# A paired product schedule with 81 instead of 90 seven-product steps, eight raw and five split tiles, and activation forms made in place

## The chip, the cores and the metric

The kernel runs on one core of one Trainium2 chip. The metric is the time of one execution on the device, in microseconds (us); a run is one execution, and the time before is the median of three.

## The reference

One encoder block on 256 tokens of width 4096, all float32:

```python
h = rms_norm(x, pre_norm_gain)
proj = h @ w_in                      # q, k, v, gate_a, indexer, z, xs, b, c, dt, merge_logits
y_a = sparse_attention(...) * silu(gate_a)          # 256 x 2048
y_b = ssd_mixer(...)                                # 256 x 2048
gates = sigmoid(merge_logits)                       # two gates of 4096 columns
merged = gates[0] * (y_a @ w_branch_attn) + gates[1] * (y_b @ w_branch_ssd)
x = x + rms_norm(merged @ w_out, post_norm_gain)
```

Nearly all arithmetic is in the four kinds of matrix product: the input projection, the merge-gate columns of it, the two branch projections and the output projection.

## The kernel before

**Splits.** Each float32 product is made of three matmuls on a split pair: a high part (ScalarE copy into `wh`, rounded) and a low part (VectorE, value minus high part, `wl`); high x high, high x low and low x high are added up in PSUM. Weights come from HBM in raw tiles of 128 x 1024 (512 KB, `raw_tile`, RBUFS = 6 of them, line 26) on SP's DMA queue; their parts go to `wh` and `wl` tiles, SBUFS = 5 of each (line 25). A raw tile is free again when both parts are made.

**The first part** (`gemm`, lines 146 to 194, up to some 1609 us) does the indexer, the attention and the state-space projections and the first two gate blocks plainly, with attention and scan work fed in between.

**The paired part** (`pair_gemm`, lines 768 to 868) does the rest but for the last two blocks of the output projection. It works on two blocks of 512 output columns at once, on both halves of the tokens and on pairs `i` of 128-row blocks of the inner dimension: a 2 x 2 by 2 x 2 block product in each step. A step is of one of two kinds:

- S, seven products (a Winograd scheme, 21 matmuls of 128 x 128 by 128 x 512, all at L786). VectorE adds weight blocks for it (L830, L835, L836) ahead of the splits (L739 and L743, a last one of 512 columns).
- D, eight products, 24 matmuls, from differences of the activations; R is the same without differences. VectorE makes two low parts (L741 for the negated one, L743).

Which pairs are S is set by SX (gates: the odd pairs), SY (branches) and SM (output projection), lines 34 to 36, and by `plain` lists in which an S pair becomes R. The groups in order of time are called here G0 to G6 (seven gate groups, 16 steps each), B00, B01, B20 ... B61 (four column pairs n, two branches, 8 steps each) and O0, O2, O4 (output projection, 16 steps each). MIXED (line 881) is the order of the pairs in G0 to G5, O2 and O4: 0 to 7, then 9, 8, 11, 10, 13, 12, 15, 14. With odd pairs as S it reads D S D S D S D S S D S D S D S D. There are 90 S steps and 134 others.

**Banks.** Eight PSUM banks take the products; after each group `turn(mode)` maps the next group's products to the banks that are emptied first (LOG, line 749). `early`, `late` and `rest` (lines 788 to 814) empty them into four SBUF tiles with VectorE; L814 subtracts product 8.

**Activations.** For each pair, `make_base` splits the activation and `make_ext` (lines 700 to 719) forms its sums or differences into a tile `f` (name frm, one buffer) and splits them. The x inputs are formed before and in G0 (`ext_x`, L912), the branch inputs in G6 and B00 (read from HBM scratch, fr from yscr on POOL's queue, two fr tiles), those of the output projection from B61 on (fr from mscr).

**What sets the order.** Side work is written as generators on one list, `aux`; `step()` takes the next piece of the list's first generator, once or twice in each product step (`pace`), and that fixes the order of the program. The framework's planner then orders each engine's queue: by program order, but work that its own estimate of times holds ready may go ahead of earlier work that it holds not ready. At run time each queue is strictly in order. The loads of the gates (`load_sig`, L963) sit in SP's queue at step 5 of each branch group; `ev_branch` multiplies with them (L968), and its last use frees their tiles.

```python
            ra, rb = raw_tile(), raw_tile()
            load_half(ra, chunk(i), 0)
            load_half(rb, chunk(i), 1)
            if n in hooks:
                hooks[n]()
            if kind == "S":
                V.tensor_add(ra[:, 0, :], ra[:, 0, :], rb[:, 0, :])
                b11, b21 = split(rb, 2)
                t1, b22 = split(ra, 2)
                V.tensor_sub(ra[:, 1, :], ra[:, 0, :], ra[:, 1, :])
                V.tensor_sub(rb, rb, ra[:, 1:2, :].to_broadcast([P, 2, NW]))
                t2, = split(ra[:, 1:2, :], 1)
                t3, t4 = split(rb, 2)
```

Of the kernel before, what the change touches and what calls it, by code (L numbers as in the profile page):

```python
# [11 lines left out]
F32 = mybir.dt.float32  # L12
# [13 lines left out]
RBUFS = 6  # L26
# [7 lines left out]
SX = tuple(range(1, 16, 2))  # L34
# [10 lines left out]
def fused_block(tc, x, xT, w_qi, w_misc, w_attn, w_ssd, w_gate0, w_gate, w_br, w_out2, w_out,  # L45
# [304 lines left out]
    def transpose4(src, dst, eng):  # L350
# [4 lines left out]
        if eng is A:  # L355
            A.activation(dst, b3, AF.Copy)
        else:
            eng.tensor_copy(dst, b3)
# [13 lines left out]
    def qi_score(j):  # L372
        for t in range(2):
            nk = (t + 1) * P
            per = NW // nk
            for h0 in range(0, 8, 2 * per):
# [6 lines left out]
                for o in range(2):  # L383
                    rl = attp.tile([P, NW], F32, tag="rl", name="rl")
# [315 lines left out]
    def make_ext(i, a, seven, diff=True):  # L700

        n = 4 if i in seven else 2
        if n == 2 and not diff:
            return
        f = tp.tile([P, n, P], F32, tag="f", name="frm")
        if n == 4:
            a11, a21 = a[:, 0, 0:P], a[:, 0, P:S]
            a12, a22 = a[:, 1, 0:P], a[:, 1, P:S]
            V.scalar_tensor_tensor(f[:, 0, :], a22, -1.0, a21, ALU.mult, ALU.subtract)
            V.tensor_sub(f[:, 2, :], a21, a11)  # L710
            V.scalar_tensor_tensor(f[:, 1, :], f[:, 0, :], -1.0, a11, ALU.mult, ALU.subtract)
            V.tensor_sub(f[:, 3, :], f[:, 1, :], a12)
        else:
            V.tensor_sub(f, a[:, :, 0:P], a[:, :, P:S])
# [11 lines left out]
    def form(i, name):  # L726
        n = int(name[1])
        if name[0] == "S":
            return ext[i][:, 0, n - 1, :], ext[i][:, 1, n - 1, :]
# [38 lines left out]
    def pair_gemm(what, mode, chunk, plan, outs, evac, hooks={}, pace=1):  # L768
# [25 lines left out]
        def late():  # L794
# [4 lines left out]
            V.tensor_add(dest[1], ps[5], dest[1])  # L799
            V.scalar_tensor_tensor(dest[3], ps[5], -1.0, dest[2], ALU.mult, ALU.subtract)  # L800

        def rest():
# [7 lines left out]
            V.scalar_tensor_tensor(c12, ps[3], -1.0, c12, ALU.mult, ALU.subtract)  # L810
            V.tensor_add(c11, ps[2], c11)
            V.tensor_add(c21, ps[4], c21)
            if 8 in ps:
                V.tensor_sub(c22, c22, ps[8])  # L814
# [7 lines left out]
        for n, (i, kind) in enumerate(plan):  # L822
# [20 lines left out]
            else:  # L843
# [7 lines left out]
                if n == after:  # L851
                    early()
                    if not left.get(5):
                        late()
                        ended.append(0)
# [9 lines left out]
        if not ended:  # L865
            pending.append(late)
# [3 lines left out]
    def forms_from(what, load, seven, pairs, diff=True):  # L870
        a = load(pairs[0])
        for i in pairs:
            ahead = load(i + 1) if i + 1 in pairs else None
            make_base(i, a)
            make_ext(i, a, seven, diff)
# [3 lines left out]


    MIXED = (0, 1, 2, 3, 4, 5, 6, 7, 9, 8, 11, 10, 13, 12, 15, 14)
# [340 lines left out]
```

## Time and profile before

| what | value |
|---|---|
| median of three runs | 2918.04 us (2916.93 to 2919.03) |
| the profiled execution's own time | 2920.13 us |
| its span, first to last instruction | 2918.4 us |
| mean granted clock of TensorE | 0.995 of full speed |
| busy: TensorE, VectorE, ScalarE | 99%, 70%, 51% of the span |
| HBM traffic | 202 GB/s over the span |

Times in the profile are counted from the start of the span. A start is measured; the end of a matmul is modelled, and matmuls overlap, so a busy share of TensorE can hide short waits. PE is TensorE, PEld its weight loads, DVE VectorE, ACT ScalarE, SP and POOL the engines whose queues issue the DMAs. L786 is line 786 of the kernel. A row of the windows gives start and end, the length, the busy time of each engine with its number of instructions in brackets (PE, PEld, DVE, ACT, POOL as far as asked for), the granted clock of TensorE, the DMA engines' busy share and GB/s; a matmul of the group before that still runs at the start is in the number.

### The profile page before, as it was taken

To read this page: it belongs to the slowest core of one execution; us is meant where nothing else is said; L and a number is where in the kernel's file an instruction comes from. 1 tells how busy PE (TensorE), PEld (TensorE's weight loads), DVE (VectorE), ACT (ScalarE), POOL (GpSimd) and SP (SyncE) were. 2 spreads that over 40 slices of the span, in tenths; PEclk is the share of its full clock that TensorE was granted. 3 is DMA by queue.
4 is the path that set the end of the run, shared out by engine and by line. 5 is a ranking of instruction groups with operands and counts; after the bars stand their busy time and mean duration, and the time that the engine had idled before them with its cause. 6 is when DMAs were issued, how large, how long until landed. Compare 5 with 4: busy or idle time off the path is not lost.

```text
span 2918.4 us, 35378 instructions
## 1 busy us (share of the span) xinstructions
PE 2878.4 (99%) x12990; PEld 2364.6 (81%) x12990; DVE 2038.7 (70%) x2494; ACT 1490.1 (51%) x1805; POOL 197.9 (7%) x202
## 2 busy tenths in 40 slices
PE   9999999999999999999999999999999999999998
PEld 7878888888888888888888778787787888887876
DVE  6677455454554556565657888888897899988975
ACT  7444444444444445455545555555565555555553
POOL 0100001000010112121301000000000000000000
PEclk9999999999999999999999999999999999999999
DMA  9545555555555455545555566665676666865674
GB/s 358 186 161 179 188 179 191 192 179 189 180 189 193 176 185 177 186 175 186 177 185 193 182 222 215 210 215 198 206 240 233 230 237 228 277 219 184 225 244 151
DMA packets 170848, 592.40 MB, mean 203 GB/s; under 512 B 19632, under 2 KB 20400, under 8 KB 170672
## 3 DMA queue, kind: packets, MB, share of 16 engines
q1 hardware_dynamic: 163728, 567.05, 56.0%
q0 software_dynamic: 6944, 23.07, 2.2%
q8 instruction: 102, 1.67, 0.2%
q14 instruction: 74, 0.61, 0.1%
HBM read 570.12 MB, written 19.92 MB: 202 GB/s over the span
## 4 chain that ended last, share of the span: by engine, by line
PE 82%; DVE 8%; DMA 6%; issue 2%; ACT 1%; SPq 0%; DVEq 0%; ACTq 0%; POOLq 0%
PE p L786 25%; PE p L186 18%; PE p L188 18%; PE p L187 18%; DMA raw<-w_gate_d 3%; DVE wl L743 3%; DMA raw<-w_out_d 1%; ACT wh L739 1%; DVE raw L836 1%; DVE wl L741 1%; DMA fr<-yscr 1%; DVE raw L830 1%; PE p L353 1%; PE p L614 0%; PE p L381 0%
## 5 line engine op out<-in xcount | busy, mean ns | idle before, releaser
L178 DVE TENSOR_TENSOR wl<-raw,wh 128x1024 fp32r<-128x1024 f32 x560 | 696.6, 1245 | 593.7 <-ACT wh L177 591.8
L177 ACT ACTIVATE wh<-raw 128x1024 fp32r<-128x1024 f32 x560 | 593.7, 1061 | 791.3 <-PE p L188 696.2
L186 PE MATMUL p<-wh,b 128*128 128x512 f32 x2304 | 910.0, 395 | 1.4 <-ACT wh L174 1.1
L187 PE MATMUL p<-wl,b 128*128 128x512 f32 x2304 | 898.4, 390 | 0.2 <-DVE wl L175 0.2
L188 PE MATMUL p<-wh,b 128*128 128x512 f32 x2304 | 898.3, 390 | 0.0
L739 ACT ACTIVATE wh<-raw 128x1024 fp32r<-128x1024 f32 (+1 forms) x628 | 600.5, 994 | 454.6 <-DVE raw L835 202.8
L786 PE MATMUL p<-wh,b 128*128 128x512 f32 x2300 | 763.6, 393 | 2.4 <-ACT wh L739 1.5
L743 DVE TENSOR_TENSOR wl<-raw,wh 128x1024 fp32r<-128x1024 f32 (+1 forms) x494 | 544.0, 1123 | 59.1 <-ACT wh L739 57.4
L786 PEld LDWEIGHTS p<-wh,b 128*128 128x128 f32 x2300 | 434.9, 189 | 97.5 <-ACT wh L739 5.7
L186 PEld LDWEIGHTS p<-wh,b 128*128 128x128 f32 x2304 | 432.6, 188 | 93.4 <-ACT wh L174 3.3
L188 PEld LDWEIGHTS p<-wh,b 128*128 128x128 f32 x2304 | 432.4, 188 | 90.8
L187 PEld LDWEIGHTS p<-wl,b 128*128 128x128 f32 x2304 | 433.1, 188 | 88.7 <-DVE wl L175 1.4
L786 PE MATMUL p<-wl,b 128*128 128x512 f32 x1150 | 450.8, 392 | 2.2 <-DVE wl L741 2.1
L786 PE MATMUL p<-wh,ext 128*128 128x512 f32 x1104 | 388.0, 392 | 0.0
L786 PEld LDWEIGHTS p<-wl,b 128*128 128x128 f32 x1150 | 217.8, 189 | 49.2 <-DVE wl L741 2.8
L786 PEld LDWEIGHTS p<-wh,ext 128*128 128x128 f32 x1104 | 208.3, 189 | 44.4 <-ACT wh L739 2.5
L786 PE MATMUL p<-wl,ext 128*128 128x512 f32 x552 | 218.5, 396 | 17.3 <-DVE wl L743 17.0
L741 DVE SCALAR_TENSOR_TENSOR wl<-raw,wh 128x1024 fp32r<-128x1024 f32 x134 | 163.5, 1220 | 12.7 <-ACT wh L739 12.7
L786 PEld LDWEIGHTS p<-wl,ext 128*128 128x128 f32 x552 | 104.1, 189 | 47.2 <-DVE wl L743 26.2
L836 DVE TENSOR_TENSOR raw<-raw 128x1024 f32<-128x1024 f32 x90 | 110.1, 1223 | 2.0
L830 DVE TENSOR_TENSOR raw<-raw 128x512 f32<-128x512 f32 x90 | 62.1, 690 | 62.7 <-DMA raw<-w_gate_d 39.6
L290 POOL TENSOR_TENSOR ro<-m,m 128x512 f32<-128x512 f32 (+1 forms) x26 | 41.9, 1621 | 412.2 <-DVE m L288 404.1
(223 smaller groups left out, 1344.3 us busy)
## 6 DMA issues: line engine op xcount, KB each, us to landing
raw<-w_attn_d SPq DMA_DIRECT2D x256, 512.0 KB, 3.6
raw<-w_gate_d SPq DMA_DIRECT2D x256, 512.0 KB, 4.3
raw<-w_ssd_d SPq DMA_DIRECT2D x192, 512.0 KB, 3.6
raw<-w_br_d SPq DMA_DIRECT2D x128, 512.0 KB, 4.7
raw<-w_out_d SPq DMA_DIRECT2D x128, 512.0 KB, 4.7
raw<-w_qi_d SPq DMA_DIRECT2D x62, 512.0 KB, 5.3
sg<-sscr SPq DMA_DIRECT2D x32, 256.0 KB, 4.0
sscr<-pc POOLq DMA_DIRECT2D x28, 256.0 KB, 2.8
```

What stands on the lines that cost most here:

```text
L177: A.activation(wh, rs, AF.Copy)
L178: V.tensor_sub(wl, rs, wh.bitcast(F32))
L186: T.matmul(ps[t], al[:, tk], wh[:, i, :], start=first, stop=False)
L187: T.matmul(ps[t], ah[:, tk], wl[:, i, :], start=False, stop=False)
L188: T.matmul(ps[t], ah[:, tk], wh[:, i, :], start=False, stop=last)
L290: G.tensor_add(ro, m1, m2)
L739: A.activation(h, src, AF.Copy, scale=float(sign))
L741: V.scalar_tensor_tensor(l, src, -1.0, fbit(h), ALU.mult, ALU.subtract)
L743: V.tensor_sub(l, src, fbit(h))
L786: T.matmul(ps[j], l, r, start=first and n == 0, stop=left[j] == 0 and n == 2)
L830: V.tensor_add(ra[:, 0, :], ra[:, 0, :], rb[:, 0, :])
L836: V.tensor_sub(rb, rb, ra[:, 1:2, :].to_broadcast([P, 2, NW]))
```

## The change

- RBUFS goes from 6 to 8; SBUFS stays at 5. Room comes from smaller buffers elsewhere: `rl` (scores), `mT` (transposed merge results of the last block pair), `og` and the last residual tile use tiles that exist already.
- SX is 1, 3, 5, 8, 10, 12, 14, and MIXED is gone: the pairs come in plain order, D S D S D S D D S D S D S D S D. O0 has an order of its own. The S steps are 7 in each of six gate groups, 3 in G6, 18 in the branches, 4, 7 and 7 in O0, O2 and O4.
- `make_ext` forms the sums in the activation's own tile, without `f`; `forms_from` takes two list steps for each pair instead of one.
- The branch inputs are started at step 4 of G6, all 16 on one generator, instead of 8 at step 8 and 8 in B00. G6 hands its banks on in the mode "aux" instead of "D".
- `late`, `rest` and the end of a group take product 8 earlier in two cases.

```diff
-RBUFS = 6
+RBUFS = 8
...
-SX = tuple(range(1, 16, 2))
+SX = (1, 3, 5, 8, 10, 12, 14)
 SY = (1, 4, 6, 9, 12, 14)
 SM = SX
...
-                    rl = attp.tile([P, NW], F32, tag="rl", name="rl")
+                    rl = yr.tile([P, NW], F32, tag=f"yr{6 + o}", name="rl")
...
     def make_ext(i, a, seven, diff=True):
 
-        n = 4 if i in seven else 2
-        if n == 2 and not diff:
+        if i not in seven and not diff:
             return
-        f = tp.tile([P, n, P], F32, tag="f", name="frm")
-        if n == 4:
-            a11, a21 = a[:, 0, 0:P], a[:, 0, P:S]
-            a12, a22 = a[:, 1, 0:P], a[:, 1, P:S]
-            V.scalar_tensor_tensor(f[:, 0, :], a22, -1.0, a21, ALU.mult, ALU.subtract)
-            V.tensor_sub(f[:, 2, :], a21, a11)
-            V.scalar_tensor_tensor(f[:, 1, :], f[:, 0, :], -1.0, a11, ALU.mult, ALU.subtract)
-            V.tensor_sub(f[:, 3, :], f[:, 1, :], a12)
+        a11, a21, a12, a22 = (a[:, k, t * P:(t + 1) * P] for k in range(2) for t in range(2))
+        if i in seven:
+            V.scalar_tensor_tensor(a22, a22, -1.0, a21, ALU.mult, ALU.subtract)
+            V.tensor_sub(a21, a21, a11)
+            V.scalar_tensor_tensor(a11, a22, -1.0, a11, ALU.mult, ALU.subtract)
+            V.tensor_sub(a12, a11, a12)
+            f, n = a.rearrange("p k (t c) -> p (k t) c", t=2), 4
         else:
-            V.tensor_sub(f, a[:, :, 0:P], a[:, :, P:S])
+            f, n = a[:, :, 0:P], 2
+            V.tensor_sub(f, f, a[:, :, P:S])
...
             V.tensor_add(dest[1], ps[5], dest[1])
+            if 8 in ended:
+                V.tensor_sub(dest[3], dest[3], ps[5])
+                return
...
             V.scalar_tensor_tensor(c12, ps[3], -1.0, c12, ALU.mult, ALU.subtract)
+            if 8 in ps and 8 not in ended:
+                V.tensor_sub(c22, c22, ps[8])
             V.tensor_add(c11, ps[2], c11)
             V.tensor_add(c21, ps[4], c21)
-            if 8 in ps:
-                V.tensor_sub(c22, c22, ps[8])
...
+                if n == len(plan) - 1 and dest and not ended and left.get(8) == 0:
+                    V.scalar_tensor_tensor(dest[3], dest[2], -1.0, ps[8], ALU.mult, ALU.subtract)
+                    ended.append(8)
...
             make_base(i, a)
+            yield
             make_ext(i, a, seven, diff)
...
-    MIXED = (0, 1, 2, 3, 4, 5, 6, 7, 9, 8, 11, 10, 13, 12, 15, 14)
...
-        plan = kinds(SX, range(16) if last else MIXED, range(8, 16) if last else ())
+        plan = kinds(SX, range(16), range(8, 16) if last else ())
...
-            push(forms_from("y", load_y, SY, range(8)))
+            push(forms_from("y", load_y, SY, range(16)))
...
-        pair_gemm("x", "D", lambda i: w_gate[g, i], plan, lambda: yr4(4 * (g % 2)), ev_gate(cols),
-                  {8: start_y} if last else {})
+        pair_gemm("x", "aux" if last else "D", lambda i: w_gate[g, i], plan, lambda: yr4(4 * (g % 2)), ev_gate(cols),
+                  {4: start_y} if last else {})
...
+            if n == 6:
+                for _ in range(4):
+                    yield
             for b in range(2):
-                mT = brp.tile([P, 4, S], F32, tag=f"mT{b if n == 6 else 0}", name="mT")
+                if (n, b) == (6, 1):
+                    m2 = [brp.tile([P, 2, S], F32, tag=f"sg{h}", name="mT") for h in range(2)]
...
+                mT = brp.tile([P, 4, S], F32, tag="mT", name="mT")
...
-            if (n, br) == (0, 0):
-                hooks[0] = lambda: push(forms_from("y", load_y, SY, range(8, 16)))
...
-            order = (0, 2, 4, 6, 1, 8, 3, 10, 5, 12, 7, 14, 9, 11, 13, 15)
-            plain = (9, 11, 13, 15)
+            order = (0, 2, 4, 6, 7, 1, 9, 3, 8, 5, 11, 10, 12, 13, 14, 15)
+            plain = (8, 10, 14)
         else:
-            order, plain = MIXED, ()
+            order, plain = range(16), ()
...
-            r = extb.tile([P, 2, NW], F32, tag=f"eb{SX[i]}", name="xr")
+            r = extb.tile([P, 2, NW], F32, tag=f"eb{SX[i]}", name="xr") if i < 7 else None
```

## Rows read from the trace of the kernel before

**Rows 1.** The page's first part: busy us (share of the span) and instructions

```profile
PE 2878.4 (99%) x12990; PEld 2364.6 (81%) x12990; DVE 2038.7 (70%) x2494; ACT 1490.1 (51%) x1805; POOL 197.9 (7%) x202
```

**Rows 2.** Windows of G6, B00, B21, B61, sum of all 18 groups, every engine

```profile
2123.85:2211.05 87.20, 86.16 (x373) 69.33 (x372) 74.59 (x111) 51.45 (x70) 9.32 (x17) 1.00 0.70 235
2211.05:2257.50 46.45, 44.34 (x193) 35.80 (x192) 33.38 (x40) 25.39 (x30) 2.73 (x5) 1.00 0.69 238
...
2342.35:2383.85 41.50, 41.50 (x184) 34.35 (x184) 38.14 (x43) 21.81 (x24) 0.00 (x0) 1.00 0.68 235
...
2512.60:2556.10 43.50, 43.50 (x193) 36.04 (x192) 37.08 (x58) 23.96 (x29) 3.29 (x6) 1.00 0.79 276
...
sum 1207.87, PE 1185.94 PEld 967.57 DVE 1056.15 ACT 670.70 POOL 34.91; mean PE 65.89 PEld 53.75 DVE 58.68 ACT 37.26 POOL 1.94
```

**Rows 3.** Windows of steps 0 to 7, L786 alone: G0, G1, sum of eight groups

```profile
1608.71:1654.07 45.36, 43.07 (x180) 34.75 (x181) 0.96 0.55 185
1696.59:1737.39 40.80, 40.80 (x181) 33.78 (x181) 1.00 0.65 226
...
sum 332.34, PE 329.77 PEld 270.92; mean PE 41.22 PEld 33.87
```

**Rows 4.** Windows of steps 8 and 9, L786 alone: G1, sum of eight groups

```profile
1737.39:1751.47 14.08, 12.52 (x46) 9.36 (x46) 0.88 0.49 169
...
sum 109.39, PE 95.36 PEld 71.17; mean PE 11.92 PEld 8.90
```

**Rows 5.** Windows of steps 10 to 15, L786 alone: G1, O4, sum of eight groups

```profile
1751.47:1782.07 30.60, 30.60 (x136) 25.34 (x136) 1.00 0.66 228
...
2783.77:2816.54 32.77, 30.92 (x136) 25.07 (x134) 1.00 0.78 262
sum 247.72, PE 245.69 PEld 202.21; mean PE 30.71 PEld 25.28
```

**Rows 6.** Groups by line and shape, VectorE in G1: busy us, mean ns, idle before

```profile
L743 DVE TENSOR_TENSOR wl<-raw,wh 128x1024 fp32r<-128x1024 f32 x32 | 37.9, 1220 | 4.1 <-ACT wh L739 4.1
L836 DVE TENSOR_TENSOR raw<-raw 128x1024 f32<-128x1024 f32 x8 | 9.8, 1224 | 0.2
L741 DVE SCALAR_TENSOR_TENSOR wl<-raw,wh 128x1024 fp32r<-128x1024 f32 x8 | 9.7, 1218 | 0.2 <-ACT wh L739 0.2
L830 DVE TENSOR_TENSOR raw<-raw 128x512 f32<-128x512 f32 x8 | 5.5, 690 | 5.4 <-DMA raw<-w_gate_d 5.4
...
L743 DVE TENSOR_TENSOR wl<-raw,wh 128x512 fp32r<-128x512 f32 x8 | 5.5, 685 | 0.0
```

**Rows 7.** Timeline of VectorE at G1's step 8: start us, us, [idle before, releaser]

```profile
1737.47 0.69 DVE L835 TENSOR_TENSOR raw<-raw 128x512 f32<-128x512 f32 x1
1739.39 0.69 DVE L830 TENSOR_TENSOR raw<-raw 128x512 f32<-128x512 f32 x1 [1.23 <-DMA raw<-w_gate_d]
1740.00 1.22 DVE L836 TENSOR_TENSOR raw<-raw 128x1024 f32<-128x1024 f32 x1
```

**Rows 8.** Timeline of TensorE in the same stretch

```profile
1740.15 0.39 PE L786 MATMUL p<-wh,ext 128*128 128x512 f32 x1
1741.87 0.50 PE L786 MATMUL p<-wl,ext 128*128 128x512 f32 x1 [1.34 <-DVE wl L743]
...
1744.41 0.63 PE L786 MATMUL p<-wh,ext 128*128 128x512 f32 x1
1744.84 0.63 PE L786 MATMUL p<-wl,b 128*128 128x512 f32 x1
```

**Rows 9.** Timeline of VectorE at G0's step 3

```profile
1626.51 0.69 DVE L830 TENSOR_TENSOR raw<-raw 128x512 f32<-128x512 f32 x1 [2.79 <-DMA raw<-w_gate_d]
```

**Rows 10.** Timeline of ScalarE in G6 and of TensorE in B00

```profile
2192.10 0.63 ACT L723 ACTIVATE b<-fr 128x512 fp32r<-128x512 f32 x1 [4.59 <-DMA fr<-yscr]
...
2212.80 0.50 PE L786 MATMUL p<-wl,b 128*128 128x512 f32 x1 [1.33 <-DVE wl L741]
...
2217.73 0.50 PE L786 MATMUL p<-wh,b 128*128 128x512 f32 x1 [0.78 <-DVE pc L814]
```

More of the change, by code (lines that the diff above doesn't have):

```diff
@@ L348, in evac_misc, with transpose4 @@
         yield
-    def transpose4(src, dst, eng):
+    def transpose4(src, dst, eng, dst2=None):
         b = aux_bank()
@@ L354, in transpose4 @@
         b3 = b.rearrange("p (i w) -> p i w", i=4)
-        if eng is A:
+        if dst2 is not None:
+            A.activation(dst, b3[:, 0:2], AF.Copy)
+            A.activation(dst2, b3[:, 2:4], AF.Copy)
+        elif eng is A:
             A.activation(dst, b3, AF.Copy)
@@ L728, in form @@
         if name[0] == "S":
-            return ext[i][:, 0, n - 1, :], ext[i][:, 1, n - 1, :]
+            n = (3, 0, 1, 2)[n - 1]
+            return ext[i][:, 0, n, :], ext[i][:, 1, n, :]
         if name[0] == "D":
@@ L854, in pair_gemm @@
                         late()
-                        ended.append(0)
+                        ended.append(5)
+                if n == len(plan) - 1 and dest and not ended and left.get(8) == 0:
+                    V.scalar_tensor_tensor(dest[3], dest[2], -1.0, ps[8], ALU.mult, ALU.subtract)
+                    ended.append(8)
                 todo = [(k, j) for j in ((5, 3, 2, 4) if kind == "D" else (3, 8, 2, 4))
@@ L864, in pair_gemm @@
             step(pace)
-        if not ended:
+        if 5 not in ended:
             pending.append(late)
@@ L977, in run @@
                 return
+            if n == 6:
+                for _ in range(4):
+                    yield
             for b in range(2):
-                mT = brp.tile([P, 4, S], F32, tag=f"mT{b if n == 6 else 0}", name="mT")
+                if (n, b) == (6, 1):
+                    m2 = [brp.tile([P, 2, S], F32, tag=f"sg{h}", name="mT") for h in range(2)]
+                    for t in range(2):
+                        transpose4(c[2 * t + b], m2[0][:, :, t * P:(t + 1) * P], A,
+                                   m2[1][:, :, t * P:(t + 1) * P])
+                        yield
+                    merged.update({14 + h: m2[h] for h in range(2)})
+                    continue
+                mT = brp.tile([P, 4, S], F32, tag="mT", name="mT")
                 for t in range(2):
@@ L1017, in open_og @@
         ogp["cm"], p = open_pool("ogp")
-        ogp["og"] = [[p.tile([P, 2, NW], F32, name=f"og{t}_{n}") for n in range(4)]
+        ogp["og"] = [[p.tile([P, 2, NW], F32, name=f"og{t}_{n}") for n in range(3)]
                      for t in range(2)]
+        ogp["o6"] = [p.tile([P, NW], F32, name=f"o6_{t}") for t in range(2)]
         ogp["oss"] = p.tile([P, 2, 8], F32, name="oss")
@@ L1062, in fused_block, with og @@
     run_pending()
-    og, oss = ogp["og"], ogp["oss"]
+    oss = ogp["oss"]
+    def og(t, n):
+        if n < 6:
+            return ogp["og"][t][n // 2][:, n % 2, :]
+        return ogp["o6"][t] if n == 6 else yr.tile([P, NW], F32, tag=f"yr{4 + t}", name="o7")
     fin_cm, fin = open_pool("fin")
@@ L1076, in run @@
                 if n < 7:
-                    V.tensor_mul(og[t][n // 2][:, n % 2, :], ps[t], pgs[n])
+                    V.tensor_mul(og(t, n), ps[t], pgs[n])
                 yield
@@ L1082, in load_x @@
         for i in range(8):
-            r = extb.tile([P, 2, NW], F32, tag=f"eb{SX[i]}", name="xr")
+            r = extb.tile([P, 2, NW], F32, tag=f"eb{SX[i]}", name="xr") if i < 7 else None
             for t in range(2):
-                res[t, i] = r[:, t, :]
+                res[t, i] = r[:, t, :] if i < 7 else tp.tile([P, NW], F32, tag="fr", bufs=2, name="xr")
                 nc.sync.dma_start(res[t, i], x[t * P:(t + 1) * P, i * NW:(i + 1) * NW])
@@ L1096, in final @@
             cs = slice(i * NW, (i + 1) * NW)
-            o = og[t][i // 2][:, i % 2, :]
+            o = og(t, i)
             if i == 7:
```

## The prediction

> **What bounds the kernel now.** I read the page's busy shares first. TensorE is busy in 99% of the span, 2878.4 of 2918.4 us, VectorE in 70% [rows 1]: it looks as if there were 40 us to be had and only on TensorE. That busy time is of no use for this change, since matmuls overlap and their ends are modelled. So I went on to the windows, one for each group of the paired part, and compared each length with its number of matmuls. Two groups show no idle time: B21, 183 matmuls of the product line (L786) in 41.50 us, and B61, 192 in 43.50 us [rows 2]. Both give **0.2267 us from one matmul to the next**, and every group should cost that times its count.
>
> Against this measure the 18 groups are long by much more than their idle time shows. They hold 90 seven-product steps of 21 matmuls and 134 eight-product steps of 24, 5106 matmuls, which at 0.2267 is 1157.5 us. They take 1207.87 us, 50.3 more, while TensorE's busy time in them, 1185.94 us, leaves 21.9 us idle [rows 2]. About 8 of the 50.3 us belong to B20, B40, B60 and O0, most of it transposes that the change keeps.
>
> Summed by idle time the change could win back at most 21.9 us and pay 6.1 (below), so it would end no lower than 15.8 us under the present, near 2902 us; summed by the spacing of the starts it has 50.3 - 8 = 42 us to work on. The Trainium skill ("Perfetto Trace Analysis", section "Identifying the Most-Contended Engine") says that matmul busy time is no good measure of TensorE's headroom, because matmuls are pipelined; by that rule 2902 us is no bound, and the 50.3 beside the 21.9 us bear it out.
>
> **Where the lost time sits.** I cut the eight groups with the mixed order (G0 to G5, O2, O4) in three: steps 0 to 7, which alternate D S D S; steps 8 and 9, where an S follows an S and then a D; steps 10 to 15, alternating again. The alternating parts of G1 take 40.80 us for 180 matmuls (due: 40.8) and 30.60 us for 135 (due: 30.6): nothing is lost [rows 3, 5]. The middle, 45 matmuls and due 10.2 us, takes 14.08 us [rows 4]. The eight middles sum to 109.39 us against 81.6 due: **27.8 us are lost where one seven-product step follows another.** The first parts lose 332.34 - 326.4 = 5.9 us, 4.6 of it in G0 [rows 3]; the last parts lose 247.72 - 244.8 = 2.9 us, 2.2 of it in O4 [rows 5]. G6 takes 87.20 us for 372 matmuls (due 84.3) and B00 46.45 us for 192 (due 43.5): 5.8 us together [rows 2].
>
> Why there: a seven-product step costs VectorE two adds of 0.69 us (L830, L835), one of 1.22 us (L836) and the low parts of the splits, three of 1.22 and one of 0.69 us: 6.95 us. An eight-product step costs 2.44 us (L741, L743) [rows 6, 7]. TensorE needs 21 x 0.2267 = 4.76 us and 5.44 us for them. A D and an S together are 9.39 us of VectorE for 10.2 of TensorE, which just fits; two S are 13.9 for 9.5, and VectorE falls 4.4 us behind. The timeline shows the second cause in the same place: L835 of the second S ends, then VectorE waits 1.23 us for the raw weights of an S **two steps further on** (L830), with L836 of the present step queued behind it [rows 7]. The six raw tiles are all taken, so that load was issued late. TensorE's starts then stand 1.72 us apart, and soon after some 0.43 us (1744.41 to 1744.84), double the pitch: the granted clock of that window is 0.88, a stretch of it at the lower of its two levels, 1.2 GHz [rows 4, 8]. That is counted in the 27.8 us.
>
> **The change, part by part.**
> 1. *Fewer seven-product steps.* The new lists give 6 x 7 + 3 in the gates, 18 in the branches, 4 + 7 + 7 in the output projection: 81. Nine steps grow from 21 to 24 matmuls: 27 x 0.2267 = **+6.1 us**, all on the path.
> 2. *No S after S, and 8 raw tiles.* Every gate group, O2 and O4 become D S D S D S D D S D S D S D S D, also across group borders. The present parts of that pattern lose next to nothing with six tiles, and the new order has a spare D in the middle. I take all of it: **-27.8 us** (bounds -27.8 and 0). VectorE's busy time in a gate group falls by 6.95 - 2.44 = 4.5 us. The eight tiles let the queue of SP issue each raw load one step earlier; nothing is moved past it.
> 3. *Start of G0.* VectorE is still forming x inputs and then waits 2.79 us in L830 for raw weights [rows 9]. Forms in place need no separate form tile (one buffer for all pairs), there are seven long forms for eight, and two more tiles bring that load earlier. I take the wait: **-2.8 us** (bounds -4.6 and 0).
> 4. *Branch inputs.* They now start at step 4 of G6 instead of 8, with two list steps for each pair, so about twelve pairs are formed in G6 and the rest in B00, for eight and eight now, and at half the pace. What is late there now: ScalarE stood 4.59 us in its queue for an input load (fr from yscr), with split work behind it; B00's first product waited 1.33 us for a low part, its seventh 0.78 us for VectorE's L814, which empties an accumulator bank [rows 10]. The bank order "aux" gives that product another bank, emptied earlier. In place, an input tile stays taken until its last low part is done, so the next load on the POOL queue (two tiles) goes out later; at half the rate this should be covered. I take **-3.5 us** (bounds -5.8, all that is lost, and +4.6, one more such wait).
> 5. *End of O4.* With no backlog from its S after S, about half of the later 2.2 us goes: **-1.0 us** (bounds -2.2 and 0). The loads of x for the residual stay in the same queue.
> 6. *Output-projection inputs.* Two list steps for each pair double the turns that pairs 0 to 7 take in B61, ahead of the branch evacuation on the list, and the hook at step 5 drains what is left. VectorE then does three pairs and four products in one go, and the four gate loads on SP, with raw loads behind them, wait for it. B61 is free of loss now [rows 2]; I take **+0.5 us** (bounds 0 and +4.6, the longest wait for an input load seen [rows 10]).
> 7. Score tiles in another pool, the transposed merge results in two half tiles (two short copies for one), smaller output tiles, the residual's last block in another tile, and L814 earlier: no instruction of weight more; covered by TensorE's matmuls, and at most the half microsecond already taken in 6 if that cover went. The new order of O0 keeps its four S apart; I take 0 (bounds -0.5 and +1).
>
> Sum: 6.1 - 27.8 - 2.8 - 3.5 - 1.0 + 0.5 = **-28.5 us**. The profiled execution took 2920.13 us, so 2891.6; it lies 2.1 us above the median of the three runs, 2918.04, which puts the forecast at **2889.5 us**. Some 0.2% (5.8 us) is what a measurement of this kernel can tell from no change.
>
> **Rivals.**
> *A. Only the order pays.* The S after S goes (-21.7 us with the added matmuls) but parts 3 to 6 give nothing: 2896 us, or up to 2905 if both waits of 4.6 us come in full. For it: input tiles are held longer in place, and ScalarE's queue has been blocked by them before. Against: half the rate.
> *B. Half of the stalls come back.* The planner that orders VectorE's queue still puts L830 ahead of L836, and each group keeps half its loss: 6.1 - 13.9 = -7.8, 2910 us. For it: that order is in the rows, and with more tiles L830 can be placed earlier still. Against: the alternating parts have the same L830 and lose nothing.
> *C. Slower.* The late raw load is the whole cause and only moves to another S in each of the eight groups: VectorE blocked in L830 once for each group, at the present 3.5 us. Then the 27.8 us stay and the 6.1 us of matmuls come on top: 2924 us. It decides once more than 21.7 of the 27.8 us, 2.7 us for each group, are still lost. Against: the middle alone is lossy, and there VectorE's deficit of 4.4 us explains it without the load.
> The Trainium skill's same section says to improve the engine with the highest occupancy first; this change adds work to that engine, and by that rule case C's 2924 us would be the result. TensorE's rows speak against it, because its waits weigh more than the added work.
>
> **How the numbers follow.** Forecast 0.62 (its own range 2882 to 2897), A 0.22, B 0.10, C 0.06. The low end is all lower bounds together, -34.3 us, and a microsecond of scatter; the high end takes in A in full and leaves out B and C. Faster by more than 0.2% takes the forecast, A and most of B: 0.90; within it 0.05; slower 0.05.
>
> **What would show it.** Right: 5133 matmuls in L786 at 0.2267 us; gate groups of 363 in about 82.3 us; no stretch at the lower clock in G1 to G5; L830 no longer waits over 1 us for raw weights. Wrong: stretches of 4 us lost behind a step whose L830 waits (B, C); a long B61 or G6 with ScalarE waiting for fr (A).

## The result, and the profile after

The changed kernel takes **2891.56 us** (median of four runs, 2890.68 to 2893.58) against 2917.48 us for the kernel before on the same chip (2913.31 to 2919.03): a ratio of 0.9914, with a 95% interval of 0.9897 to 0.9932, or 25.9 us less. The forecast was 2889.5 us, range 2882 to 2905. The profiled execution took 2891.08 us, against 2920.13 us before: 29.05 us less, and the terms below are compared with that one.

The first part of the page, as in [rows 1], shows 27 matmuls more and VectorE with 38.7 us less to do:

```profile
PE 2867.5 (99%) x13017; PEld 2368.0 (82%) x13017; DVE 2000.0 (69%) x2441; ACT 1471.9 (51%) x1788; POOL 197.6 (7%) x202
```

The windows of the groups, every engine, as in [rows 2]: G1, G3, G6, B00, B61, O4 and the sum of all 18.

```profile
1691.91:1774.94 83.03, 82.76 (x364) 67.97 (x364) 70.92 (x75) 46.00 (x51) 2.16 (x4) 1.00 0.65 218
...
1857.54:1939.82 82.28, 82.28 (x364) 68.13 (x364) 71.41 (x75) 46.34 (x51) 2.16 (x4) 1.00 0.64 214
...
2104.38:2190.44 86.06, 85.32 (x376) 70.31 (x376) 72.08 (x105) 49.81 (x67) 8.74 (x16) 1.00 0.71 239
2190.44:2237.58 47.14, 44.41 (x193) 35.88 (x193) 31.96 (x41) 24.92 (x31) 3.26 (x6) 1.00 0.71 242
...
2492.23:2535.75 43.52, 43.52 (x193) 36.04 (x192) 37.38 (x56) 24.78 (x30) 3.28 (x6) 1.00 0.84 295
...
2704.20:2787.71 83.51, 82.75 (x364) 67.96 (x364) 73.07 (x80) 45.93 (x55) 0.00 (x0) 1.00 0.73 243
sum 1178.08, PE 1173.57 PEld 969.10 DVE 1016.08 ACT 652.75 POOL 34.77; mean PE 65.20 PEld 53.84 DVE 56.45 ACT 36.26 POOL 1.93
```

A gate group now has 363 matmuls, due 363 x 0.2267 = 82.29 us; G3 takes 82.28, and so do G0, G4, G5 and O2. The 18 groups take 1178.08 us for 5133 matmuls. At 0.2267 us each that is 1163.7 us, so 14.4 us lie above the pace where 50.3 lay before, about 8 of them in both cases the transposes and other matmuls between. TensorE's idle time fell from 21.9 to 4.5 us (1178.08 - 1173.57), by 17.4 us; the loss against the pace fell by 35.9. In what follows a "loss" is a window's length less its matmuls of the product line times 0.2267 us.

The granted clock is 1.00 in every one of the 18 windows; before, six of them read 0.98. The two steps after the seventh of each group (steps 8 and 9), product line alone, as in [rows 4]: G1, and the sum of the eight groups.

```profile
1733.39:1743.77 10.38, 10.38 (x46) 8.36 (x45) 1.00 0.57 195
...
sum 81.78, PE 81.78 PEld 67.48; mean PE 10.22 PEld 8.44
```

That is 81.78 us for 109.39, with 81.6 due. Nearly all the time came from here.

One row speaks against the reasons given for it. From the page's list of groups, first the changed kernel's first weight add (L836, L830 before): busy, mean ns, then VectorE's idle time ahead of it and what ended most of that.

```profile
L836 DVE TENSOR_TENSOR raw<-raw 128x512 f32<-128x512 f32 x81 | 55.8, 689 | 66.3 <-DMA raw<-w_gate_d 38.0
```

The same row of the kernel before:

```profile
L830 DVE TENSOR_TENSOR raw<-raw 128x512 f32<-128x512 f32 x90 | 62.1, 690 | 62.7 <-DMA raw<-w_gate_d 39.6
```

VectorE still stands at the head of its queue waiting for raw weights, 66.3 us in 81 adds where it was 62.7 in 90. The timeline of VectorE in the changed kernel has single waits twice as long as the 1.23 us of [rows 7], in G1 and in O4 (start us, us, [idle before, releaser]):

```profile
1739.31 0.69 DVE L836 TENSOR_TENSOR raw<-raw 128x512 f32<-128x512 f32 x1 [2.58 <-DMA raw<-w_gate_d]
...
2732.75 0.69 DVE L836 TENSOR_TENSOR raw<-raw 128x512 f32<-128x512 f32 x1 [2.46 <-DMA raw<-w_out_d]
```

So the wait did not go; it all but stopped costing: G1, G2 and O4 lose 0.7, 0.3 and 1.2 us, the other five of the eight groups nothing. The other place where a term failed is B00. TensorE's timeline there, the rows that answer to [rows 10]:

```profile
2196.50 0.50 PE L789 MATMUL p<-wh,b 128*128 128x512 f32 x1 [1.78 <-DVE pc L804]
...
2210.47 0.50 PE L789 MATMUL p<-wl,b 128*128 128x512 f32 x1 [0.95 <-DVE wl L744]
```

The seventh product now waits 1.78 us for L804, which empties another bank, where it waited 0.78 us for L814. And ScalarE waits longer for the branch inputs. The view of tile fr on ScalarE in the changed kernel, from 2100 to 2230 us: the splits of the sixteen inputs with first and last start, then idle us until the input load had landed, and how often.

```profile
L725 ACT ACTIVATE b<-fr x16: 616/632/633, 2110.1 to 2207.4; 128x512 fp32r<-128x512 f32 x16
...
  DMA fr<-yscr: 32.9, 13
```

The same for the kernel before:

```profile
L723 ACT ACTIVATE b<-fr x16: 614/632/636, 2129.5 to 2220.7; 128x512 fp32r<-128x512 f32 x16
...
  DMA fr<-yscr: 15.1, 8
```

### The profile page after: what moved, and what is told of

The parts are those of the page before. It is cut to its first block, busy times and chain, and to the rows that moved or that the text cites. A ratio compares the mean times of both kernels' runs of the same rounds, so it can differ in the third digit from the quotient of the medians.

```text
span 2889.3 us, 35364 instructions
## 1 busy us (share of the span) xinstructions
PE 2867.5 (99%) x13017; PEld 2368.0 (82%) x13017; DVE 2000.0 (69%) x2441; ACT 1471.9 (51%) x1788; POOL 197.6 (7%) x202
## 4 chain that ended last, share of the span: by engine, by line
PE 75%; issue 19%; DVE 2%; DMA 2%; POOL 1%; ACT 0%; SPq 0%; POOLq 0%; DVEq 0%; ACTq 0%
PE p L789 18%; PE p L186 18%; PE p L188 18%; PE p L187 18%; DMA fr<-yscr 1%; PE p L353 1%; PE p L617 1%; POOL sscr L911 1%; PE p L384 0%; DVE wl L178 0%; DVE wl L746 0%; PE p L475 0%; PE p L448 0%; PE p L607 0%; DVE og L1125 0%
## 5 line engine op out<-in xcount | busy, mean ns | idle before, releaser
L742 ACT ACTIVATE wh<-raw 128x1024 fp32r<-128x1024 f32 (+1 forms) x610 | 584.3, 997 | 424.0 <-DVE raw L841 203.7
L746 DVE TENSOR_TENSOR wl<-raw,wh 128x1024 fp32r<-128x1024 f32 (+1 forms) x467 | 515.6, 1127 | 56.3 <-ACT wh L742 55.7
L789 PE MATMUL p<-wh,ext 128*128 128x512 f32 x1060 | 369.5, 389 | 0.0
L789 PEld LDWEIGHTS p<-wh,ext 128*128 128x128 f32 x1060 | 198.9, 188 | 41.3
L789 PE MATMUL p<-wl,ext 128*128 128x512 f32 x530 | 206.6, 390 | 1.0 <-DVE wl L746 1.0
L744 DVE SCALAR_TENSOR_TENSOR wl<-raw,wh 128x1024 fp32r<-128x1024 f32 x143 | 174.3, 1219 | 12.0 <-ACT wh L742 11.7
L836 DVE TENSOR_TENSOR raw<-raw 128x512 f32<-128x512 f32 x81 | 55.8, 689 | 66.3 <-DMA raw<-w_gate_d 38.0
L842 DVE TENSOR_TENSOR raw<-raw 128x1024 f32<-128x1024 f32 x81 | 99.0, 1222 | 2.0
```

The costliest lines, as they stand in the source:

```text
L742: A.activation(h, src, AF.Copy, scale=float(sign))
L744: V.scalar_tensor_tensor(l, src, -1.0, fbit(h), ALU.mult, ALU.subtract)
L746: V.tensor_sub(l, src, fbit(h))
L789: T.matmul(ps[j], l, r, start=first and n == 0, stop=left[j] == 0 and n == 2)
```

## The experiments

Three theories were put to the test for the 27.8 us of the middles. **Theory 1**, the prediction's: two S steps in a row put VectorE 4.4 us behind, and that deficit is the cause. **Theory 2**: the late raw load is, and eight raw tiles cure it. **Theory 3**, formed after the first four runs (trials 1, 2, 3 and 7): the order of VectorE's queue is the cause, in which the planner puts the first add of a later S, with its wait for a raw load, ahead of the work of the present S. The kernel before has somewhat different medians on the chips of the trials (2923.3, 2920.4 and 2927.8 us), so ratios, or kernels run together, are compared. The changed kernel itself, run again beside them, stood at 0.9908 [0.9894, 0.9923] and 0.9896 [0.9882, 0.9911].

**1. The order without the raw tiles** (beside 2923.3 us). The changed kernel with six raw tiles:

```diff
-RBUFS = 8
+RBUFS = 6
```

> The changed kernel with six raw tiles instead of eight; all else as changed. Theory 1 (the loss came from VectorE, which needs 13.9 us for two seven-product steps that take TensorE 9.5): the order alone brings the gain, so 2891 us within 3 us, gate groups G1 to G5 at 82.3 us within 0.8. Theory 2 (the late raw load was the cause, and the two more tiles cured it): most of the 27.8 us come back, 2910 to 2919 us, each gate group 85 us or more.

Measured: 2897.13 us (2893.23 to 2906.73), ratio 0.9913 [0.989, 0.9937], as with eight. That is 6 us over theory 1's figure, on a chip where the kernel before is 5 us slower too. The losses of G1 to G5 were 1.4 (theory 1 allowed 0.8), 0, 0.1, 0 and 0 us. The row of the first add:

```profile
L836 DVE TENSOR_TENSOR raw<-raw 128x512 f32<-128x512 f32 x81 | 55.6, 687 | 33.6 <-DMA raw<-w_out_d 16.5
```

With six tiles the wait is **half** of what it is with eight, 33.6 us for 66.3. The new tiles are not the cure of the middles, and theory 2 falls. Nor is the wait by itself the cost: the changed kernel has twice as much of it and loses as little in the middles. Elsewhere this trace is worse: G6 lost 6.0 us, for 1.1 to 2.0 in three executions of the changed kernel. Whether the tiles help there was not tested by itself; trial 5, with eight, lost more in G6 still.

**2 and 3. An S after an S put back, with eight and with six raw tiles.** Eighty-one S steps and the changed forms stay; only the order of pairs in G0 to G5, O2 and O4 is altered, so that it reads D S D S D S D S S D D S D D S D.

```diff
-        plan = kinds(SX, range(16), range(8, 16) if last else ())
+        plan = kinds(SX, range(16) if last else (0, 1, 2, 3, 4, 5, 6, 8, 10, 7, 9, 12, 11, 13, 14, 15), range(8, 16) if last else ())
...
-            order, plain = range(16), ()
+            order, plain = (0, 1, 2, 3, 4, 5, 6, 8, 10, 7, 9, 12, 11, 13, 14, 15), ()
```

> The changed kernel with eight raw tiles, but in G0 to G5, O2 and O4 the pairs come in an order with two seven-product steps in a row at steps 7 and 8 (D S D S D S D S S D D S D D S D); the same number of matmuls. Theory 1: each of the eight groups loses 2.5 to 4 us at step 8 again, 20 to 32 us in all, 2911 to 2923 us. Theory 2: the eight tiles prevent it, at most 0.5 us for each group, 2892 to 2896 us.

> Both parts undone: the order with two seven-product steps in a row at steps 7 and 8, and six raw tiles; the same number of matmuls as the changed kernel. Theory 1: as with eight tiles, 20 to 32 us more than the changed kernel, and not over 6 us more than the run with eight tiles and that order. Theory 2: 28 us more than the changed kernel, and 20 us or more above the run with eight tiles.

Measured with eight tiles: 2906.25 us (2902.96 to 2909.06), 0.9939 [0.9919, 0.9959]. Steps 8 and 9, product line alone, in G1 and in all eight groups:

```profile
1735.18:1746.78 11.60, 10.89 (x46) 8.22 (x46) 1.00 0.54 155
...
sum 95.45, PE 87.98 PEld 65.69; mean PE 11.00 PEld 8.21
```

Measured with six: 2903.13 us (2900.69 to 2904.95), 0.9929 [0.9912, 0.9945]. The same view:

```profile
1735.00:1745.58 10.58, 10.58 (x46) 8.31 (x46) 1.00 0.59 194
...
sum 85.54, PE 85.11 PEld 66.27; mean PE 10.64 PEld 8.28
```

The same order, matmuls and VectorE work lose 95.45 - 81.6 = 13.9 us with eight tiles and 3.9 with six. With theory 1 both would lose some 28, and with theory 2 the eight tiles would be the better. What differs is the order of VectorE's queue. Its timeline in G1, with eight tiles:

```profile
1735.61 0.69 DVE L836 TENSOR_TENSOR raw<-raw 128x512 f32<-128x512 f32 x1 [0.54 <-DMA raw<-w_gate_d]
1736.22 0.69 DVE L841 TENSOR_TENSOR raw<-raw 128x512 f32<-128x512 f32 x1
1736.94 1.23 DVE L842 TENSOR_TENSOR raw<-raw 128x1024 f32<-128x1024 f32 x1
```

With six, in the same place:

```profile
1733.66 1.22 DVE L746 TENSOR_TENSOR wl<-raw,wh 128x1024 fp32r<-128x1024 f32 x1 [0.67 <-ACT wh L742]
1734.92 0.69 DVE L841 TENSOR_TENSOR raw<-raw 128x512 f32<-128x512 f32 x1
1735.65 1.23 DVE L842 TENSOR_TENSOR raw<-raw 128x1024 f32<-128x1024 f32 x1
```

With eight tiles the add of a later S (L836), waiting for its load, stands ahead of the second S's own second and wide add (L841, L842); with six it does not. In the trace with six tiles no first add that waits stands ahead of the present step's adds anywhere in G0 to G5, O2 and O4; in the kernel before one stands there in every one of the eight middles, with waits of 0.59 to 2.02 us. That made theory 3, and the next trial tested it with nothing else altered.

**4. One ordering edge in the kernel before** (beside 2920.4 us, and once more beside 2927.8). Ninety S steps, six raw tiles, MIXED order, forms and buffers all as before. The first add of an S may not be queued ahead of the last low part of the S before it:

```diff
+    low, behind = [None], [None]
...
-            V.tensor_sub(l, src, fbit(h))
+            low[0] = V.tensor_sub(l, src, fbit(h))
...
-                V.tensor_add(ra[:, 0, :], ra[:, 0, :], rb[:, 0, :])
+                with tc.issue_after(behind[0]) if behind[0] is not None else nullcontext():
+                    V.tensor_add(ra[:, 0, :], ra[:, 0, :], rb[:, 0, :])
...
                 t3, t4 = split(rb, 2)
+                behind[0] = low[0].ins
```

> The kernel before, unchanged in order, steps and buffers, but the first weight add of a seven-product step (L830) may not stand ahead of the last low part of the seven-product step before it in VectorE's queue. Theory 1 (VectorE's 4.4 us deficit over two seven-product steps in a row): the loss at steps 8 and 9 stays, 3 us or more for each of the eight groups, total within 5 us of the kernel before. Theory 3 (the add of a later step, placed ahead by the planner, waits for its load and holds up the adds of the present step): the loss falls to 1 us or less for each group, total 20 to 30 us less than before, 2893 to 2903 us where before is 2923.

Measured: **2891.61 us** (2888.55 to 2895.25), 0.9897 [0.9882, 0.9912], 28.8 us under the kernel before. Steps 8 and 9, product line alone, in G1 and in all eight groups:

```profile
1731.76:1742.37 10.61, 10.61 (x46) 8.30 (x46) 1.00 0.57 177
...
sum 86.25, PE 85.33 PEld 66.22; mean PE 10.67 PEld 8.28
```

The 14.08 us of [rows 4] became 10.61, the 109.39 became 86.25, and the S after S are all still there. The first add's row in the page (now L833) and VectorE's timeline at the second S of G1:

```profile
L833 DVE TENSOR_TENSOR raw<-raw 128x512 f32<-128x512 f32 x90 | 61.5, 683 | 4.8 <-DMA raw<-w_out_d 2.7
```

```profile
1731.69 0.69 DVE L838 TENSOR_TENSOR raw<-raw 128x512 f32<-128x512 f32 x1
1732.41 1.23 DVE L839 TENSOR_TENSOR raw<-raw 128x1024 f32<-128x1024 f32 x1
...
1738.26 0.68 DVE L833 TENSOR_TENSOR raw<-raw 128x512 f32<-128x512 f32 x1
```

Second add and wide add now follow each other, the later S's first add comes 4.6 us after them, when its weights have landed, and the 62.7 us of waits are 4.8. Theory 3 is shown. What S after S costs by itself is what is left: (86.25 - 81.6) / 8 = 0.6 us a group, 1.8 of the 4.65 us in O4, more than the 1 us that theory 3 allowed a group, and 0.4 in each of the others.

**5. The same edge in the changed kernel** (beside 2920.4 us).

> The changed kernel with the same rule for the first weight add. Theory 3: what the changed kernel still loses behind such waits (G1, G2 and O4, about 2 us) goes, the rest stays: 0 to 3 us less than the changed kernel. Theory 1: no difference. A loss would show that early adds are of use.

Measured: 2891.24 us (2891.16 to 2893.88), 0.9897 [0.9883, 0.9912], where the changed kernel run with it took 2895.07 (2892.11 to 2898.23): 3.8 us less, with ranges that overlap. G0 to G5, O2 and O4 lose nothing at all, where the changed kernel beside it lost 5.7 us in them, but its profiled execution, the longest of its runs, loses 8.9 us in G6 (375 matmuls, due 85.0):

```profile
2102.59:2196.51 93.92, 88.29 (x376) 70.89 (x375) 72.63 (x107) 50.42 (x67) 9.28 (x17) 0.99 0.67 220
```

ScalarE waited 36.7 us for fr loads there. Its other three runs took 2.6 us less; whether the edge had a part in this loss was not told apart (trial 1, without the edge, lost 6.0 us there).

**6. Ninety S steps and the edge in the changed kernel** (beside 2920.4 us): the changed forms, with SX the odd pairs again, MIXED order, O0's old order, and seven raw tiles.

```diff
-RBUFS = 8
+RBUFS = 7
...
-SX = (1, 3, 5, 8, 10, 12, 14)
+SX = tuple(range(1, 16, 2))
```

> The changed kernel with the seven-product steps and the orders of the kernel before (90 steps, the mixed order, seven raw tiles for want of room) and the rule for the first weight add. Theory 3: 27 matmuls less than the changed kernel, 6.1 us, and no loss at steps 8 and 9 over 0.5 us for each group: 3 to 6 us less than the changed kernel. Theory 1: 3 us or more lost in each of the eight groups, 18 us or more above the changed kernel.

A miss. Measured: 2898.17 us (2897.37 to 2898.68), 0.9918 [0.9901, 0.9934], 3.1 us more than the changed kernel beside it. The middles sum to 87.31 us, about as in trial 4, but O0 takes 92.60 us, 6.4 more than in the changed kernel, and G6 loses 4.5. TensorE's timeline in O0:

```profile
2547.67 0.80 PE L791 MATMUL p<-wl,b 128*128 128x512 f32 x1 [3.41 <-DVE wl L748]
```

VectorE's timeline ahead of that low part:

```profile
2540.97 0.69 DVE L816 TENSOR_TENSOR pc<-pc,p 128x512 f32<-128x512 f32 x1
2541.58 1.89 DVE L981 TENSOR_TENSOR pc<-pc,sg 128x512 f32<-128x512 f32 x3
2543.39 1.28 DVE L983 TENSOR_TENSOR pc<-pc 128x512 f32<-128x512 f32 x2
2544.59 0.68 DVE L981 TENSOR_TENSOR pc<-pc,sg 128x512 f32<-128x512 f32 x1
2545.19 1.28 DVE L983 TENSOR_TENSOR pc<-pc 128x512 f32<-128x512 f32 x2
2546.40 1.22 DVE L748 TENSOR_TENSOR wl<-raw,wh 128x1024 fp32r<-128x1024 f32 x1
```

Five and a half microseconds of B61's closing work (emptying banks, gate products, their sums) stood in one piece ahead of the split. Why it does so here and not in the changed kernel was not tried.

**7. The banks of G6** (beside 2923.3 us). The changed kernel with the plain bank order ahead of B00, for the wait on L804:

```diff
-        pair_gemm("x", "aux" if last else "D", lambda i: w_gate[g, i], plan, lambda: yr4(4 * (g % 2)), ev_gate(cols),
+        pair_gemm("x", "D", lambda i: w_gate[g, i], plan, lambda: yr4(4 * (g % 2)), ev_gate(cols),
```

> The changed kernel with G6 handing on its banks in the mode D, as before the change, instead of aux. In the changed kernel B00's seventh product waits 1.78 us for VectorE to empty the bank of product 5; in mode D it takes the bank of product 8, which the changed code empties at G6's last step. Theory 1 (the bank decides): that wait goes, B00 is 1.5 to 2.1 us shorter, in all 2889 to 2891 us. Rival (VectorE is late there whatever the bank): a wait of the same size at another product of B00's first two steps, B00 at 47.1 us within 0.5.

Measured: 2896.33 us (2895.76 to 2897.63), 0.9906 [0.9892, 0.9921], no different from the changed kernel. The wait moved to another emptying instruction and did not shrink (TensorE's timeline in B00):

```profile
2203.67 0.50 PE L789 MATMUL p<-wh,b 128*128 128x512 f32 x1 [2.10 <-DVE pc L820]
```

B00 took 46.09 us, between what the two expected; that is a loss of 2.6 us, and it was 3.6, 2.3 and 3.5 us in three profiled executions of the changed kernel: a share of the bank order is within that scatter. With either order VectorE is late with the bank that is asked for.

**8. Forms on their old timetable** (beside 2927.8 us). Formed in place, but all within one list step, from step 8 of G6 with eight pairs, the others in B00:

```diff
             make_base(i, a)
-            yield
             make_ext(i, a, seven, diff)
...
-            push(forms_from("y", load_y, SY, range(16)))
+            push(forms_from("y", load_y, SY, range(8)))
...
-                  {4: start_y} if last else {})
+                  {8: start_y} if last else {})
...
+            if (n, br) == (0, 0):
+                hooks[0] = lambda: push(forms_from("y", load_y, SY, range(8, 16)))
```

> The changed kernel with the old schedule of the branch and output inputs: eight pairs from step 8 of G6, eight in B00, one list step for each pair; still formed in place. The prediction's part 4 (spreading them saves 3.5 us): G6 and B00 lose 3 to 5 us more than in the changed kernel (4.7 and 4.0 us in its two traces). Rival (they wait for their loads whatever the pace): within 1.5 us of it.

Measured: 2899.72 us (2898.85 to 2901.53), 0.9908 [0.9893, 0.9923], against 2896.16 (2895.23 to 2898.78) for the changed kernel beside it. G6 lost 1.4 us and B00 4.9:

```profile
2198.04:2246.45 48.41, 44.49 (x192) 36.00 (x193) 33.81 (x46) 26.88 (x33) 3.81 (x7) 1.00 0.70 234
```

Together 6.3 us, where three executions of the changed kernel lost 4.7, 4.0 and 5.5. Spreading the forms out is worth 0.8 to 2.3 us. The 3 to 5 us of the prediction's part 4 are missed against each of the three; against the execution beside it the rival holds.

**9. A third input tile** (beside 2927.8 us). The changed kernel with three fr tiles for two, and seven raw tiles for the room (the first line stands for all four places that make an fr tile):

```diff
-        a = tp.tile([P, 2, S], F32, tag="fr", bufs=2, name="fr")
+        a = tp.tile([P, 2, S], F32, tag="fr", bufs=3, name="fr")
...
-RBUFS = 8
+RBUFS = 7
```

> The changed kernel with three input tiles (fr) instead of two, and seven raw tiles to make room. If the branch inputs are late because a tile stays taken until its last low part, and the next load starts only then: G6 and B00 lose 2 us or less together, for 4.7 and 4.0, and ScalarE waits under 2 us for each input load. If the load itself or VectorE's order is what is late: the same as in the changed kernel within 1 us.

Measured: 2898.84 us (2896.85 to 2899.92), 0.9905 [0.9889, 0.9922]. B00 has no loss left, and ScalarE's wait for fr is down from 32.9 us to 12.8:

```profile
2197.18:2240.70 43.52, 43.52 (x193) 36.04 (x193) 26.90 (x32) 21.95 (x25) 2.17 (x4) 1.00 0.64 216
```

```profile
  DMA fr<-yscr: 12.8, 6
```

G6 and B00 lose 1.5 us together. The whole kernel gains nothing by it: G2 to G5, with seven raw tiles and another order out of the planner, lost 0.9 to 3.7 us each, and which of the two did that was not tried.

**10. The kernel before with the edge against the changed kernel, run together** (beside 2927.8 us): the kernel of trial 4 again.

> The changed kernel again, timed in more rounds beside the three others of this chip: 0.991 of the kernel before.

> The kernel before with the first weight add held behind the last low part of the seven-product step before it, timed in more rounds. It has 27 matmuls less than the changed kernel (6.1 us) and lost 0.7 us more in the paired part than the changed kernel in their last two traces (12.3 and 11.6): 2 to 6 us less than the changed kernel if that holds, the same within 2 us if the loss at the branch inputs eats it up.

Measured: 2896.16 us (2895.23 to 2898.78) for the changed kernel, and **2891.2 us** (2888.61 to 2892.26) for the kernel before with the edge, 0.9877 [0.9862, 0.9891]. The ranges do not meet: one edge alone beats the change by 5.0 us, near the 6.1 us of its 27 matmuls. Beside trial 4 it was 3.5 us, with ranges that overlap. In that trace the paired part takes 1176.69 us, against 1181.04.

The changed kernel run again beside trials 4 to 6 had this expectation:

> The changed kernel itself, beside the other runs of this chip: 0.991 of the kernel before; waits of VectorE for raw weights in the first weight add again of 5 us and more for each gate group, without loss on TensorE in most groups.

Its 2895.07 us and ratio of 0.9908 confirm the result; its paired part takes 1181.01 us. The part on the waits held in four of the six full gate groups: G2 to G5 have 8.1 to 9.5 us of them, G0 and G1 2.6 and 4.7, G6 next to none. G0 and G1 lose nothing, G2 to G5 0.4 to 1.3 us each.

## Why the prediction was right, and where its reasons were not

The size was right: -28.5 us forecast, -29.05 in the profiled execution, -25.9 between the medians. That the sum comes so close is in part luck: terms 3, 4 and 5 were off by -1.8, +2.4 and -0.7 us, and these cancel. By its terms, in us:

| term | forecast | measured |
|---|---|---|
| 1, 27 more matmuls | +6.1 | +6.1 |
| 2, the eight middles | -27.8 | -27.6 |
| 3, start of G0 | -2.8 | -4.6 |
| 4, branch inputs, G6 and B00 | -3.5 | -1.1 |
| 5, end of O4 (here with its first part) | -1.0 | -1.7 |
| 6, output-projection inputs, B61 | +0.5 | 0 |
| other residues in the paired part | 0 | -0.9 |
| TensorE starts the paired part later | 0 | +0.9 |
| behind the paired part | 0 | -0.2 |

**Term 1** holds to the hundredth: G3 has three matmuls more than G1 before and takes 82.28 us. The summing by start spacing held; the summing by idle time, which bounded the new time at 2902 us, did not. The Trainium skill ("Perfetto Trace Analysis", section "Identifying the Most-Contended Engine") warns of matmul busy time as a measure, and these traces agree, 17.4 us of idle time having gone beside 35.9 us of loss. The prediction's other use of it, that to improve the engine of highest occupancy first would make 2924 us of this change, does not follow: the change gives TensorE 6.1 us of work and takes 35.9 us of loss off the same engine in the paired part (50.3 to 14.4, the 6.1 counted as due).

**Term 2** is right in size, and the step behind it failed: "there VectorE's deficit of 4.4 us explains it without the load". The deficit alone costs 0.4 us a group outside O4 (trial 4). The second cause that the prediction saw in [rows 7], the first add queued ahead of L836 of the present step, is the one that has to be there too. Set out by the two, the eight middles lost:

| | a later S's first add waits ahead of the present one's | none does |
|---|---|---|
| S after S | 27.8 (before), 13.9 (trial 2) | 4.65 (trial 4), 3.9 (trial 3) |
| no S after S | 0.2, 2.6 and 1.2 (changed, its three traces; such a wait in all 24 middles) | 0 (trials 1 and 5) |

Either cure is enough, or nearly. This reading fits all four: VectorE runs some microseconds ahead of TensorE; an S after an S uses that lead up, and then a wait at the head of its queue falls on TensorE in full; with a D to follow the lead is there and the same wait is swallowed. No trial varied the lead by itself, but the rows bear out both halves. With S after S, the wait of the add that stands ahead and the loss of the middle, in us, and the granted clock there:

| | G0 | G1 | G2 | G3 | G4 | G5 | O2 | O4 |
|---|---|---|---|---|---|---|---|---|
| before: wait | 0.69 | 1.23 | 1.89 | 0.59 | 1.92 | 1.30 | 1.56 | 2.02 |
| before: loss | 1.56 | 3.88 | 4.49 | 1.46 | 4.48 | 3.89 | 4.04 | 3.99 |
| before: clock | 1.00 | 0.88 | 0.88 | 1.00 | 0.88 | 0.88 | 0.88 | 1.00 |
| trial 2: wait | 1.13 | 0.54 | 0.25 | 1.22 | 0.00 | 0.53 | 2.13 | 1.10 |
| trial 2: loss | 1.99 | 1.40 | 1.14 | 2.10 | 0.84 | 1.38 | 3.00 | 2.00 |
| trial 2: clock | 1.00 | 1.00 | 1.00 | 1.00 | 1.00 | 1.00 | 1.00 | 1.00 |

In trial 2 the loss is the wait plus 0.84 to 0.90 us in every group. In the kernel before the same sum gives G0 and G3; the five groups at 0.88 lose 1.6 to 1.8 us more, and 12% of their some 14 us is 1.7. (O4, at full clock, loses 1.8 us even without a wait, trial 4.) In G1 the starts show both: a gap of 1.72 us for 0.23 is 1.5 us, and the lower clock that followed is 1.7 of the 3.88 [rows 4, 8].

Without S after S, in the three traces of the changed kernel, thirteen of the 24 waits are 0.45 to 2.45 us long, and nothing is lost behind any of them; of the eleven from 2.56 to 3.57 us six lose 0.2 to 1.3 us. The lead there is thus some 2.5 us, an estimate from these waits. In G5, where nothing is lost, an S with a D ahead of it has the same wait in the same place (VectorE's timeline in the changed kernel):

```profile
2035.82 0.69 DVE L836 TENSOR_TENSOR raw<-raw 128x512 f32<-128x512 f32 x1 [1.24 <-DMA raw<-w_gate_d]
2036.43 0.68 DVE L841 TENSOR_TENSOR raw<-raw 128x512 f32<-128x512 f32 x1
```

It follows that rivals B and C named the right mechanism and the wrong outcome. The planner does still put the add ahead, and with more tiles earlier still, as B feared: 66.3 us against 33.6 with six. B's argument on the other side, that the alternating parts have the same add and lose nothing, decided it, though in the kernel before the adds that waited there mostly stood behind the present step's adds (waits of 1.47 and 1.19 us in G1's first part), so that the likeness was less than it seemed. The sign "L830 no longer waits over 1 us" failed outright, with single waits of 2.58 us. The eight tiles, put down as a help, are none in the middles (trial 1), and with S after S they do harm (trials 2 and 3). Why the planner places the add there was not tried.

**Term 3** was mis-sized. G0's first part lost 4.56 us [rows 3], and now nothing: all of it goes, for which the lower bound of -4.6 stood. The 2.79 us of [rows 9] left out what came after that stall. Neither reason given was needed: the first part of G0 takes its due 40.80 us with the old forms and six raw tiles once the edge is there (trial 4), and with the new forms and six tiles, where no add waits ahead (trial 3). The wait of [rows 9] stood ahead of the present step's wide add, as in the middles.

**Term 4** was mis-sized, and its step "at half the rate this should be covered" failed. The rate hardly fell: ScalarE splits the sixteen inputs over 97.3 us, for 91.2 before, and the first of them 5.7 us after the start of G6 in both kernels, whatever the step at which the program starts them. The last comes 17.0 us into B00, for 9.7 before. In place, an input tile is held until its last low part, and ScalarE's waits for fr doubled, 15.1 to 32.9 us. Trial 9 gives the tile back and the loss of G6 and B00 falls to 1.5 us, so this is the cause of most of it (seven raw tiles came with it). With the edge and the old forms the two groups lose 3.2 and 3.5 us (trials 4 and 10), less than with the change. "Emptied earlier", of the bank, failed too: the wait grew from 0.78 to 1.78 us on another instruction (trial 7). Rival A spoke of exactly this part, but its full price, two waits of 4.6 us, did not come.

**Term 5** gave -1.7 us with O4's first part. **Term 6** cost nothing: B61 takes 43.52 us for 43.5. What no term had is the 0.9 us by which TensorE comes later to the paired part, after a start of the kernel at the lower clock (below). **Rival C** asked for more than 2.7 us a group still lost, and each of the eight groups loses 0 to 1.2.

What the 27 matmuls bought could be had for less: trials 4 and 10 keep the ninety S steps; they lose 18.1 and 19.2 us in the paired part (1175.56 and 1176.69 less 1157.5), where the changed kernel lost 14.4 to 17.3 in three executions, and save the 6.1.

## What to carry to other kernels

When an in-order engine is late, look at what stands at the head of its queue and not only at how much work it has: an instruction that a planner put early, and that waits for a load, holds up ready work of the present step, and one ordering edge removed 23 of the 27.8 us lost there. A deeper pool of prefetch tiles can make this worse, because the planner then moves the waiting instruction earlier still. Cost the loss as length less matmuls times the spacing of their starts, not as idle time, and when a change gains by avoiding a place rather than by mending it, mend it in the kernel before as a trial: the gain may be had without the change's price.

## What the runs showed of the hardware

The lower clock had a share of its own in the loss: 12% of the five middles at 0.88 is some 8.6 of the 27.8 us. Six of the paired part's groups had a mean clock of 0.98 before, and all 18 read 1.00 with the stalls gone. In the kernel before, a wait of TensorE as short as that of [rows 8], 1.72 us from start to start, was followed by starts 0.43 us apart, which is 1.2 GHz for the 2.4 GHz of the 0.2267 us.

In the changed kernel TensorE's wait of 1.78 us in B00 left the clock at 1.00. The windows around it, product line alone:

```profile
2194.00:2196.00 2.00, 0.72 (x4) 0.26 (x2) 1.00 0.80 305
2196.00:2199.00 3.00, 2.50 (x11) 2.08 (x12) 1.00 0.53 183
2199.00:2202.00 3.00, 3.00 (x15) 2.49 (x14) 1.00 0.84 242
```

A longer stall went with the full clock here, as did all eight stalls of trial 2, and a shorter one with the lower clock there; what decides it, no run here shows.

The first matmuls of the changed kernel's profiled execution stood 0.43 us apart up to about 12 us, and the paired part started 0.9 us later, at 1609.63 us for 1608.71. In the kernel before they stood some 0.23 us apart from about 8 us on. This was not followed up; in the traces of the trials the paired part starts between 1608.8 and 1611.3 us.
